# Six edits joined in a one-layer hybrid encoder: order at the start, bias tiles, residual rows, sine halves, sums of W_down

## The chip, the cores and the metric

The kernel runs on one core of a Trainium2 chip. TensorE (PE in the profile; PEld is its weight load) multiplies, VectorE (DVE) and ScalarE (ACT) move results out of PSUM and do the element work, GpSimd (POOL) does element work on SBUF and issues some DMAs, and SyncE (SP) issues most DMAs. Each engine runs its own queue of instructions in order. The metric is the time of one execution in microseconds (us), as the median of several runs; smaller is better.

## The reference

One encoder layer is applied to two inputs with shared weights, `x_sample` (512 rows) and `x_prompt` (1024 rows), each with 16 meta tokens in front. Width is 1024, the MLP has 4096 channels.

```python
def encoder_layer(x, ...):
    h = rmsnorm(x, g_mix)
    z = h @ w_in
    q, k, v, u, gate_na, gate_fn = jnp.split(z, ...)
    y_na = neighbourhood_attention(q, k, v, rel_bias, meta_bias) @ w_branch_na
    y_fn = fourier_mix(u) @ w_branch_fn
    mixed = jax.nn.sigmoid(gate_na) * y_na + jax.nn.sigmoid(gate_fn) * y_fn
    x = x + mixed @ w_out
    a = jax.nn.relu(rmsnorm(x, g_mlp) @ w_up)
    return x + (a * a) @ w_down
```

Attention has 8 heads of 64. A grid token sees a window of 8 rows by 16 columns of the 64-column grid with a relative bias, and all meta tokens. `fourier_mix` is the real part of a 2-D DFT over positions and the channels of each of four groups. At the end comes an RMSNorm, and the meta rows are dropped.

## The kernel before

All products are in float32, as three passes of float32r matmuls: each operand is split into a high part (a cast, mostly on ACT) and a low part (a subtraction on POOL or DVE), and `mm3` (L125) adds high x high, high x low and low x high in PSUM. `weights` (L145) is the usual way in: one DMA on SP, the cast on ACT, the low part on POOL unless told otherwise.

The program is written in Python without hardware loops. A scheduler orders every engine's queue when the kernel is built: by program order as priority, and by when it believes that an instruction is ready. Two helpers bend that order: `mark` (L103) finds the last instruction traced on some engines, and `behind` (L118) puts what follows behind them on the same engine; `pinned` (L114) does so for all engines. All waits between engines are made by the framework from the tiles that are read and written.

`run` (L350) does the sample first and then the prompt. For the sample:

- **Start** (L363 to L380). `read` (L277) loads the meta rows and four tiles of 128 rows through three buffers, norms each (ACT squares, DVE scales), and PE transposes it into `hT`. Value weights come in four quarters of 256 rows (`value_weights`, L299), their low parts on DVE. `qk_weights(0)` (L303) brings the first keys' and queries' weights, `tables` (L201) loads a window table, subtracts a mask and stores bias tables `g` in DRAM. `project_v` (L307) multiplies the meta rows first and then the four tiles and stores the values to DRAM (`vd`).
- **Attention** (`attention`, L513). `spread_v` (L753) copies the stored values within DRAM into the windows' order. `project(0)` (L537) makes keys and queries of the first pair of heads; its matmuls are lines L531 to L533. A `unit` (L628) fetches a bias tile (`bias`, L769: one or two DMAs from `g` and a POOL copy), does scores (L647, L648), softmax (L652 to L656), transposes (L660) and the product with the values (L680). Bias loads of head 0 stand behind `spread_v` on SP.
- **Gates** (`gates`, L783). One product per weight tile; a list `beside` names generators that take one step after each product, from the first number to before the second. `fold_u` (L248) multiplies the DFT over channels into W_u: its first step loads, its eight others use PE (L259) and store. `fold_positions` (L877) adds and subtracts mirrored positions.
- **merge_na** (L820): eight weight tiles of `w_na`, through two buffers `relu`; `fn_ahead` (L847) makes ready the other branch's weights. Then `fourier_channels` (L972), `fourier_positions` (L1033) with cosine and sine tables from DRAM (`sines`, L1026, one DMA on POOL's queue), and `merge_fn` (L915), which also begins to load `w_out`.
- **project_out** (L1084) loads the residual rows `acc`, adds the product with W_out and norms; `Up.run` (L1197) does W_up in 16 pairs of products. Beside them `reading` loads, norms and transposes the prompt's rows, one tile for each pair.

The prompt goes the same way; then `Halves` (L1223) does project_out and W_up, and `down` (L1610) does W_down for both inputs in a Strassen scheme of seven quarter products. A step `(n, u)` is product n with slice u of eight; it has six row tiles of six matmuls. `load(i)` (L1636) makes step i's weights: sums of up to four quarters on DVE (L1642), then the splits. In the last slice of a product, `evict` (L1711) takes each bank out, and `load(i + 2)` follows all six.

Of the kernel before, what the change touches and what calls it, by code (L numbers as in the profile page):

```python
# [17 lines left out]
F32 = mybir.dt.float32  # L18
# [8 lines left out]
D = 1024  # L27
# [41 lines left out]
class Layer:  # L69
    def __init__(self, tc, ctx, ins, outs):  # L70
# [16 lines left out]
        nc.sync.dma_start(self.sgn, ins["sgn"])  # L87
        self.small = ctx.enter_context(tc.tile_pool(name="small", bufs=4))
        self.wpool = ctx.enter_context(tc.tile_pool(name="w", bufs=2))
        self.wv = {}  # L90
        self.meta_values = None
# [109 lines left out]
    def tables(self, marks):  # L201
# [15 lines left out]
        with self.behind(marks):  # L217
            nc.sync.dma_start(mask, self.ins["colmask"])
            nc.sync.dma_start(win, self.ins["rel_win"])
# [78 lines left out]

    def value_weights(self, q, to=None, lo_engine=None, raw="raw"):  # L299
        return self.weights(self.ins["w_in"][q * 256:(q + 1) * 256, VC:VC + 512].rearrange("(kt p) c -> p kt c", p=128), to,  # L300
                            lo_engine=lo_engine, raw=raw)

    def qk_weights(self, pr, to=(None, None)):  # L303
        return (self.weights(self.rows("w_in", KCOL + pr * 128), to[0], lo_engine=self.nc.vector if pr else None),
                self.weights(self.rows("w_in", QC + pr * 128), to[1], scale=-DH ** -0.5))

    def project_v(self, name, T, hT, p, wv):  # L307
# [12 lines left out]
        for t in range(-1 if meta is None else 0, T // 128):  # L320
# [3 lines left out]
            self.mm3(ps[:n, :], [(hT[0][:, kt, pos:pos + n], hT[1][:, kt, pos:pos + n],  # L324
                                  wv[kt // 2][0][:, kt % 2, :], wv[kt // 2][1][:, kt % 2, :]) for kt in range(8)])
            vs = p.tile([128, 512], F32R, name="pt0", tag="pt0", bufs=self.ptb).bitcast(F32)
            nc.vector.tensor_copy(vs[:n], ps[:n])
# [22 lines left out]
    def run(self, order):  # L350
# [6 lines left out]
        for i, (name, T) in enumerate(order):  # L357
# [5 lines left out]
            if i == 0:  # L363
                with pool("first", "right") as p:
                    gain = p.tile([128, D], F32, name="gain")
                    reading = self.read(name, T, hT, lambda: p.tile([128, D], F32, name="xt", bufs=3),
                                        lambda: p.tile([128, D], F32, name="hn", bufs=2), gain)
                    next(reading)
                    next(reading)
                    for q in range(4):  # L370
                        next(reading, None)
                        self.wv[q] = self.value_weights(q, self.pair(p, [128, 2, 512], bufs=4), self.nc.vector, ("raw", "raw", "hi", "lo")[q])
                    marks = self.mark((mybir.EngineType.SP,))
                    w0 = self.qk_weights(0)

                    rest = self.tables(marks)
                    for _ in reading:
                        pass
# [40 lines left out]
            if small:  # L419
                wide = lambda: [fn.tile([128, n], F32R, name=f"wu{n}")[:, :1040].rearrange("p (a b) -> p a b", a=4) for n in (1040, 1072)]  # L420
                flat = lambda pair: [t.rearrange("p a b -> p (a b)") for t in pair]
                beside = [(self.fold_u(mp.tile([128, 512], F32, name="relu", bufs=2)[:, :128],
# [1448 lines left out]
```

## Time and profile before

| | us |
|---|---|
| runs | 1922.71, 1923.19, 1925.18 |
| median | 1923.19 |
| the profiled execution's own time | 1927.61 |
| its span, first to last instruction | 1925.8 |

The profile is of one execution. Part 1 of its page gives the busy time of each engine, the chain of waits goes back from the last instruction through whatever released each step, and a table of waits says for which engine's instruction or which DMA an engine stood idle (total us, times, longest). In rows of the timeline the first two numbers are start and duration in us, and the bracket is the idle time before and what ended it; "SPq" is a DMA issue on SP. Matmuls are pipelined, so the distance between starts and not the duration is a matmul's cost. Over the whole span the granted TensorE clock was 0.998 of full speed, and the DMAs moved 358.38 MB.

### The profile page before, as it was taken

The page shows a single profiled execution, that of the slowest core. Times are in us where ns is not written, and L with a number is a line of the kernel's source. Part 1 is how long each engine was busy: PE and PEld are TensorE (multiplying, and loading weights), DVE is VectorE, ACT ScalarE, POOL GpSimd, SP SyncE. Part 2 cuts the span into 40 slices and gives each one's busy share as a digit, 9 for nine tenths or more (in the row PEclk, how much of TensorE's full clock was granted, in tenths as well). Part 3 has the DMA queues.
Part 4 walks back from the last instruction along what each step waited for, and adds up shares of the span by engine and source line. Part 5 has one row for each costly group of instructions (what it writes and reads, how often), then busy time and mean ns, then how long its engine had stood idle before and what let it go on. Part 6 is the DMA issues. An engine that isn't in the chain of part 4 may idle for free.

```text
span 1925.8 us, 26107 instructions
## 1 busy us (share of the span) xinstructions
PE 1892.8 (98%) x9435; PEld 1588.0 (82%) x9435; DVE 1117.8 (58%) x1749; ACT 753.1 (39%) x1351; POOL 816.5 (42%) x674
## 2 busy tenths in 40 slices
PE   7999999999999999999999999999999999999998
PEld 5888888888888888888898878888888888888886
DVE  5771554787625567660427376656665326758856
ACT  3674333443315556541223234333333333333434
POOL 1335543455422233342233218887882323323531
PEclk9999999999999999999999999999999999999999
DMA  6757873687756455463452523444446778567733
GB/s 221 192 152 236 232 218 124 208 271 251 237 191 173 121 145 156 120 233 105 117 158 85 175 99 121 158 173 164 173 155 250 269 250 285 207 218 281 277 118 127
DMA packets 312945, 358.38 MB, mean 186 GB/s; under 512 B 51768, under 2 KB 222392, under 8 KB 312264
## 3 DMA queue, kind: packets, MB, share of 16 engines
q1 hardware_dynamic: 295056, 334.93, 53.0%
q0 software_dynamic: 17760, 21.80, 5.0%
q8 instruction: 74, 1.21, 0.3%
q14 instruction: 55, 0.45, 0.1%
HBM read 263.06 MB, written 96.16 MB: 187 GB/s over the span
## 4 chain that ended last, share of the span: by engine, by line
PE 89%; DMA 4%; DVE 2%; issue 2%; POOL 1%; ACT 1%; SPq 0%; POOLq 0%; DVEq 0%; ACTq 0%
PE ps_mm L132 23%; PE ps_o L132 22%; PE ps_s L132 19%; PE ps_t L132 11%; PE ps_mm L531 3%; PE ps_mm L532 3%; PE ps_mm L533 3%; PE ps_o L680 2%; PE ps_t L660 1%; DMA relu<-in_w_na 1%; DMA bm<-g_un 1%; DMA sin<-in_sin_prompt 1%; PE ps_s L648 1%; PE ps_s L647 1%; PE ps_t L194 0%
## 5 line engine op out<-in xcount | busy, mean ns | idle before, releaser
L157 POOL TENSOR_TENSOR w_lo<-w_raw,w_hi 128x1024 fp32r<-128x1024 f32 x69 | 177.1, 2567 | 217.9 <-ACT w_hi L155 151.9
L157 POOL TENSOR_TENSOR w_lo<-raw,w_hi 128x1024 fp32r<-128x1024 f32 (+1 forms) x49 | 100.0, 2044 | 202.1 <-ACT w_hi L155 196.2
L155 ACT CAST w_hi<-w_raw 128x1024 fp32r<-128x1024 f32 x88 | 92.5, 1051 | 180.1 <-PE ps_s L132 58.5
L157 DVE TENSOR_TENSOR h_lo<-long,h_hi 128x1024 fp32r<-128x1024 f32 x54 | 77.1, 1428 | 94.1 <-ACT h_hi L155 94.1
L531 PE MATMUL ps_mm<-hT,w_hi 128*128 128x512 f32 (+2 forms) x296 | 121.5, 410 | 0.0
L532 PE MATMUL ps_mm<-hT,w_hi 128*128 128x512 f32 (+2 forms) x296 | 110.4, 373 | 0.0
L533 PE MATMUL ps_mm<-hT,w_lo 128*128 128x512 f32 (+2 forms) x296 | 110.4, 373 | 0.0
L155 ACT CAST h_hi<-long 128x1024 fp32r<-128x1024 f32 x54 | 56.7, 1050 | 101.6 <-PE ps_s L132 25.1
L654 ACT ACTIVATE sc<-sc,ast 128x288 f32<-128x288 f32 (+4 forms) x96 | 53.9, 561 | 68.3 <-DVE ast L652 68.0
L155 ACT CAST w_hi<-raw 128x1024 fp32r<-128x1024 f32 (+1 forms) x49 | 40.9, 840 | 100.9 <-DVE raw L1642 54.4
L157 DVE TENSOR_TENSOR hs_lo<-short,hs_hi 128x512 fp32r<-128x512 f32 x54 | 72.3, 1339 | 13.9 <-ACT hs_hi L155 11.7
L1421 POOL TENSOR_TENSOR x<-w_hi,x 128x512 fp32r<-128x512 f32 (+1 forms) x39 | 64.9, 1663 | 18.4 <-ACT x L1418 18.4
L680 PEld LDWEIGHTS ps_o<-pt,vb 104*64 104x64 f32 (+6 forms) x576 | 62.4, 163 | 9.7 <-POOL vb L617 2.6
L132 PE MATMUL ps_t<-gate,x 128*128 128x512 f32 x276 | 66.5, 390 | 0.0
L533 PEld LDWEIGHTS ps_mm<-hT,w_lo 128*128 128x128 f32 x296 | 55.7, 188 | 10.4
L680 PE MATMUL ps_o<-pt,vb 104*64 104x128 f32 (+6 forms) x576 | 62.1, 243 | 1.9 <-POOL vb L617 1.2
L617 POOL TENSOR_TENSOR vb<-vr,vb 96x384 fp32r<-96x384 f32 (+4 forms) x48 | 48.6, 1031 | 34.7 <-ACT vb L616 34.7
L132 PE MATMUL ps_mm<-gate,x 128*128 128x512 f32 x256 | 63.2, 389 | 0.0
L774 POOL MEMSET bm<- 64x96 f32 (+2 forms) x64 | 11.2, 175 | 117.1 <-DVE ast L652 101.7
L132 PEld LDWEIGHTS ps_t<-gate,x 128*128 128x128 f32 x276 | 51.7, 188 | 10.9 <-ACT w_hi L136 0.2
L652 DVE CUSTOM_DVE_ANT_0 sc<-ps_s,bm 128x288 f32<-128x288 f32 (+4 forms) x96 | 46.4, 483 | 23.6 <-issue 10.7
L532 PEld LDWEIGHTS ps_mm<-hT,w_hi 128*128 128x128 f32 x296 | 56.2, 190 | 1.6
(714 smaller groups left out, 5574.4 us busy)
## 6 DMA issues: line engine op xcount, KB each, us to landing
long<-hidden_prompt SPq DMA_DIRECT2D x54, 512.0 KB
w_raw<-in_w_in SPq DMA_DIRECT2D x52, 512.0 KB
raw<-in_w_down SPq DMA_DIRECT2D x39, 512.0 KB
w_raw<-in_w_up SPq DMA_DIRECT2D x34, 512.0 KB
hidden_prompt<-h SPq DMA_DIRECT2D x32, 512.0 KB
short<-hidden_sample SPq DMA_DIRECT2D x54, 256.0 KB
w_lo<-in_w_down SPq DMA_DIRECT2D x18, 512.0 KB
w_raw<-in_w_out SPq DMA_DIRECT2D x16, 512.0 KB
```

Source lines behind the costliest of these rows:

```text
L132: self.nc.tensor.matmul(out, a, b, start=(i == 0 and not more), stop=(i == len(terms) - 1), skip_group_check=more)
L155: nc.scalar.copy(out=hi, in_=raw)
L157: (lo_engine or nc.gpsimd).tensor_tensor(out=lo, in0=raw, in1=hi.bitcast(F32), op=ALU.subtract)
L531: nc.tensor.matmul(ps, a[0], b[0], start=(kt == 0), stop=False)
L532: nc.tensor.matmul(ps, a[0], b[1], start=False, stop=False)
L533: nc.tensor.matmul(ps, a[1], b[0], start=False, stop=(kt == 7))
L617: nc.gpsimd.tensor_tensor(out=lo, in0=vs, in1=hi.bitcast(F32), op=ALU.subtract)
L647: nc.tensor.matmul(ps[:, :W], qs[hh][:, qc], ks[hh][:, 0, kw[0], kw[1]], start=True, stop=False)
L652: nc.vector.tensor_tensor_reduce(out=sc[:, :W], in0=ps[:, :W], in1=bm[:, :W], scale=1.0, scalar=3e38, op0=ALU.add, op1=ALU.min, accum_out= ...
L654: nc.scalar.activation(out=sc[:, :W], in_=sc[:, :W], func=AF.Exp, bias=st[:, 0:1], scale=-1.0, accum_out=st[:, 1:2])
L680: nc.tensor.matmul(po[:m, j * 128:(j + 1) * 128], v, x, start=(i == 0), stop=(i == len(ops) - 1))
L1421: (engine or self.nc.gpsimd).tensor_tensor(out=w[1], in0=raw, in1=w[0].bitcast(F32), op=ALU.subtract)
```

## The change

1. At the start `read` is replaced for the sample by `read_first`: the first 128 rows are SP's first load, the meta rows come after, row tiles 2 and 3 land in key buffers, and norms and splits are written out in one order. The load of `sgn` goes behind these loads. `project_v` does the meta rows next to last: high and low parts of their 16 columns side by side in one 48-column operand, 16 matmuls in place of 24, and one add. The keys' low part is on DVE behind the last transposes.
2. `first_bias` brings the bias tiles of the first six units ahead of the last values' store.
3. `fold_u` skips the step after the second gate product and ends one product later.
4. The residual rows' loads move from `project_out` to behind `fourier_positions`, pinned. The prompt's rows in `Up.run` are pinned too.
5. The prompt's second sine table is loaded in two halves of columns.
6. In `down`, the sums for the step after next are written between the evictions.

```diff
@@ -84,10 +84,10 @@
...
-        nc.sync.dma_start(self.sgn, ins["sgn"])
@@ -215,6 +215,7 @@
...
         with self.behind(marks):
+            nc.sync.dma_start(self.sgn, self.ins["sgn"])
             nc.sync.dma_start(mask, self.ins["colmask"])
@@ -296,12 +297,66 @@
...
+    def read_first(self, name, T, hT, gain, p, more):
...
+        xs, hns, raws = {}, {}, {}
+        def load(t):
+            n = NM if t < 0 else 128
+            xs[t] = p.tile([128, D], F32, name="xt", bufs=3) if t < 2 else more()
+            nc.sync.dma_start(xs[t][:n], self.ins["meta_tokens"] if t < 0 else self.ins[f"x_{name}"][t * 128:(t + 1) * 128, :])
+        def load_w(q):
+            raws[q] = self.wtile(("raw", "raw", "hi", "lo")[q], [128, 2, 512]).bitcast(F32)
+            nc.sync.dma_start(raws[q], self.value_rows(q))
+        def norm(t):
+            n = NM if t < 0 else 128
+            hns[t] = p.tile([128, D], F32, name="hn", bufs=2)
+            self.norm(xs[t][:n], gain, hns[t][:n], n)
+        def turn(t):
+            self.transpose_in(hns[t], hT, 0 if t < 0 else self.lead + t * 128, NM if t < 0 else 128)
+        def split(q):
+            self.wv[q] = self.split_sb(raws[q], *self.pair(p, [128, 2, 512], bufs=4), lo_engine=nc.vector)
+        load(0)
+        self.gain(gain, "g_mix")
+        load_w(0)
+        load(1)
+        load_w(1)
+        load(-1)
+        load_w(2)
+        load_w(3)
+        for t in range(2, T // 128):
+            load(t)
+        norm(0)
+        turn(0)
+        split(0)
+        norm(1)
+        split(1)
+        split(2)
+        turn(1)
+        split(3)
+        with self.behind(self.mark((mybir.EngineType.Activation, mybir.EngineType.DVE))):
+            norm(2)
+            turn(2)
+            for t in (-1, 3):
+                norm(t)
+                turn(t)
+    def value_rows(self, q):
+        return self.ins["w_in"][q * 256:(q + 1) * 256, VC:VC + 512].rearrange("(kt p) c -> p kt c", p=128)
...
-    def qk_weights(self, pr, to=(None, None)):
-        return (self.weights(self.rows("w_in", KCOL + pr * 128), to[0], lo_engine=self.nc.vector if pr else None),
...
+    def qk_weights(self, pr, to=(None, None), late=()):
+        return (self.weights(self.rows("w_in", KCOL + pr * 128), to[0], lo_engine=self.nc.vector if pr or late else None, lo_marks=late),
                 self.weights(self.rows("w_in", QC + pr * 128), to[1], scale=-DH ** -0.5))
@@ -317,14 +372,35 @@
...
-        for t in range(-1 if meta is None else 0, T // 128):
+        order = list(range(T // 128))
+        for t in order if meta is not None else order[:-1] + [-1] + order[-1:]:
+            if meta is None and t == T // 128 - 1:
+                with self.behind(self.mark((mybir.EngineType.SP,))):
+                    self.first_bias(p, T)
...
             ps = self.psum()
-            self.mm3(ps[:n, :], [(hT[0][:, kt, pos:pos + n], hT[1][:, kt, pos:pos + n],
-                                  wv[kt // 2][0][:, kt % 2, :], wv[kt // 2][1][:, kt % 2, :]) for kt in range(8)])
+            if t < 0:
+                own = p.tile([128, 512], F32R, name="pt1", tag="pt1", bufs=self.ptb)[:, :8 * 48].rearrange("p (k c) -> p k c", k=8)
+                nc.gpsimd.tensor_copy(own[:, :, NM:2 * NM].rearrange("p k (g c) -> p k g c", c=8),
+                                      self.zero[:, None, None, 0:8].to_broadcast([128, 8, 2, 8]))
+                for i in range(2):
+                    nc.scalar.copy(out=own[:, :, 32 * i:32 * i + NM], in_=hT[i][:, :, 0:NM].bitcast(F32))
+                for i in range(2):
+                    for kt in range(8):
+                        nc.tensor.matmul(ps[:48], own[:, kt], wv[kt // 2][i][:, kt % 2, :], start=(kt + i == 0), stop=(kt + i == 8))
+            else:
+                self.mm3(ps[:n, :], [(hT[0][:, kt, pos:pos + n], hT[1][:, kt, pos:pos + n],
+                                      wv[kt // 2][0][:, kt % 2, :], wv[kt // 2][1][:, kt % 2, :]) for kt in range(8)],
+                         late="b" if meta is None and t < 2 else "a")
             vs = p.tile([128, 512], F32R, name="pt0", tag="pt0", bufs=self.ptb).bitcast(F32)
-            nc.vector.tensor_copy(vs[:n], ps[:n])
+            if t < 0:
+                low = p.tile([128, 512], F32R, name="pt1", tag="pt1", bufs=self.ptb).bitcast(F32)[:n]
+                nc.scalar.copy(out=low, in_=ps[32:32 + n])
+                nc.vector.tensor_tensor(out=vs[:n], in0=ps[:n], in1=low, op=ALU.add)
+            else:
+                nc.vector.tensor_copy(vs[:n], ps[:n])
@@ -363,19 +439,12 @@
...
-                    reading = self.read(name, T, hT, lambda: p.tile([128, D], F32, name="xt", bufs=3),
-                                        lambda: p.tile([128, D], F32, name="hn", bufs=2), gain)
-                    next(reading)
-                    next(reading)
-                    for q in range(4):
-                        next(reading, None)
-                        self.wv[q] = self.value_weights(q, self.pair(p, [128, 2, 512], bufs=4), self.nc.vector, ("raw", "raw", "hi", "lo")[q])
+                    self.read_first(name, T, hT, gain, p, lambda: att.tile(
+                        [128, 2, T // 64 + 2, 64], F32R, name="k", tag="k", bufs=4).rearrange("p i a b -> p (i a b)").bitcast(F32)[:, :D])
                     marks = self.mark((mybir.EngineType.SP,))
-                    w0 = self.qk_weights(0)
+                    w0 = self.qk_weights(0, late=self.mark((mybir.EngineType.DVE,)))
                     rest = self.tables(marks)
@@ -419,10 +488,10 @@
...
-                beside = [(self.fold_u(mp.tile([128, 512], F32, name="relu", bufs=2)[:, :128],
+                beside = [self.fold_u(mp.tile([128, 512], F32, name="relu", bufs=2)[:, :128],
                                        [t.bitcast(F32) for _ in range(2) for t in flat(self.pair(mp, [128, 2, 512]))],
-                                       lambda: flat(self.pair(fn, [128, 4, 128], bufs=4))), 0, 9),
-                          (fold, 5, 13)]
+                                       lambda: flat(self.pair(fn, [128, 4, 128], bufs=4)))]
+                beside = [(*beside, 0, 1), (*beside, 2, 10), (fold, 5, 13)]
@@ -454,6 +523,10 @@
             with self.pinned():
                 for _ in ahead:
                     pass
+                if small:
+                    acc = [ap.tile([128, D], F32, name=f"acc{t}") for t in range(T // 128)]
+                    for t in range(T // 128):
+                        nc.sync.dma_start(acc[t], self.ins[f"x_{name}"][t * 128:(t + 1) * 128, :])
@@ -501,6 +573,15 @@
...
+    def first_bias(self, p, T):
+        blocks = row_blocks(T // 64)
+        wide = max(b["n"] * w for b in blocks for w in KW)
+        for u in range(6):
+            h, R, j = u // (4 * len(blocks)), u // 4 % len(blocks), u % 4
+            self.bms.append(p.tile([128, wide], F32, name="bm", bufs=6))
+            self.bias(self.bms[-1], h, j, KW[j], blocks[R])
@@ -637,9 +718,12 @@
...
-            bm = p.tile([128, wide], F32, name="bm", bufs=6 if T == 512 else 4)
-            with self.behind(spread if h == 0 else []):
-                self.bias(bm, h, j, w, b)
+            if self.bms:
+                bm = self.bms.pop(0)
+            else:
+                bm = p.tile([128, wide], F32, name="bm", bufs=6 if T == 512 else 4)
+                with self.behind(spread if h == 0 else []):
+                    self.bias(bm, h, j, w, b)
@@ -1027,7 +1111,9 @@
...
-        self.nc.gpsimd.dma_start(t, self.ins[f"sin{i}_{name}"].rearrange("(t p) k -> p t k", p=128))
+        src = self.ins[f"sin{i}_{name}"].rearrange("(t p) k -> p t k", p=128)
+        for ks in (slice(0, 262), slice(262, R + 1)) if i and R > 512 else (slice(0, R + 1),):
+            self.nc.gpsimd.dma_start(t[:, :, ks], src[:, :, ks])
@@ -1081,14 +1167,12 @@
...
         gain = self.gain(p.tile([128, D], F32, name="gain", bufs=1), "g_mlp")
-        for t in range(nt):
-            nc.sync.dma_start(acc[t], x[t * 128:(t + 1) * 128, :])
@@ -1217,7 +1301,8 @@
...
                 if g:
-                    next(reading, None)
+                    with layer.pinned():
+                        next(reading, None)
@@ -1634,12 +1719,17 @@
...
         def load(i):
+            for _ in load_parts(i):
+                pass
+        def load_parts(i):
             if i >= len(steps):
                 return
             rs, rl, rw, *rest = (x.bitcast(F32) for x in self.raws.pop(i))
             n, u = steps[i]
             for x, (_, sign) in zip(rest, self.parts(self.DOWN[n][1], u)[1:]):
                 nc.vector.tensor_tensor(out=rw, in0=rw, in1=x, op=ALU.add if sign > 0 else ALU.subtract)
+                yield
@@ -1767,13 +1857,21 @@
...
+            loading, sums = iter(()), 0
+            if u == nu - 1 and i + 2 < len(steps):
+                loading = load_parts(i + 2)
+                sums = len(self.parts(self.DOWN[n + 1][1], 1)) - 1
             for t in range(nh):
                 product(banks[t], t, n, [u])
                 if u == nu - 1:
                     evict(n, t)
+                    if t < sums:
+                        with layer.pinned():
+                            next(loading, None)
             with layer.pinned():
                 if u == nu - 1:
-                    load(i + 2)
+                    for _ in loading:
+                        pass
```

More of the change, by code (lines that the diff above doesn't have):

```diff
@@ L90, in __init__ @@
         self.wv = {}
+        self.bms = []
         self.meta_values = None
@@ L297, in read @@
         self.transpose_in(*last)
+    def read_first(self, name, T, hT, gain, p, more):
+        nc = self.nc
+        xs, hns, raws = {}, {}, {}
[38 more added lines that the diff above has]
+                turn(t)
@@ L299, in value_weights @@
+    def value_rows(self, q):
+        return self.ins["w_in"][q * 256:(q + 1) * 256, VC:VC + 512].rearrange("(kt p) c -> p kt c", p=128)
     def value_weights(self, q, to=None, lo_engine=None, raw="raw"):
-        return self.weights(self.ins["w_in"][q * 256:(q + 1) * 256, VC:VC + 512].rearrange("(kt p) c -> p kt c", p=128), to,
-                            lo_engine=lo_engine, raw=raw)
-    def qk_weights(self, pr, to=(None, None)):
-        return (self.weights(self.rows("w_in", KCOL + pr * 128), to[0], lo_engine=self.nc.vector if pr else None),
+        return self.weights(self.value_rows(q), to, lo_engine=lo_engine, raw=raw)
@@ L365, in run @@
                     gain = p.tile([128, D], F32, name="gain")
-                    reading = self.read(name, T, hT, lambda: p.tile([128, D], F32, name="xt", bufs=3),
-                                        lambda: p.tile([128, D], F32, name="hn", bufs=2), gain)
-                    next(reading)
-                    next(reading)
-                    for q in range(4):
-                        next(reading, None)
-                        self.wv[q] = self.value_weights(q, self.pair(p, [128, 2, 512], bufs=4), self.nc.vector, ("raw", "raw", "hi", "lo")[q])
+                    self.read_first(name, T, hT, gain, p, lambda: att.tile(
+                        [128, 2, T // 64 + 2, 64], F32R, name="k", tag="k", bufs=4).rearrange("p i a b -> p (i a b)").bitcast(F32)[:, :D])
                     marks = self.mark((mybir.EngineType.SP,))
-                    w0 = self.qk_weights(0)
+                    w0 = self.qk_weights(0, late=self.mark((mybir.EngineType.DVE,)))
                     rest = self.tables(marks)
-                    for _ in reading:
-                        pass
                     self.project_v(name, T, hT, att, self.wv)
@@ L480, in run @@
                 continue
-            acc = [ap.tile([128, D], F32, name=f"acc{t}") for t in range(T // 128)]
             self.short = mlp = self.Up(self, ap, hp_, mp, name, T, h2T)
@@ L485, in run @@
                 rest = list(wout)
-            self.project_out(hp_, mp, self.ins[f"x_{name}"], T, h2T, rest, acc, mlp, marks)
+            self.project_out(hp_, mp, T, h2T, rest, acc, mlp, marks)
             out.close()
@@ L1082, in out_weights, with project_out @@
             yield self.weights(src, place and (place() if callable(place) else self.pair(*place)), lo_engine=self.nc.vector if i == 2 else None)
-    def project_out(self, hp, p, x, T, m, wo, acc, mlp, marks):
+    def project_out(self, hp, p, T, m, wo, acc, mlp, marks):
         nc = self.nc
```

## The prediction

> **What bounds the kernel now.** First the page, part 1, then the waits of PE alone, then the chain of waits for the pace of a matmul.
>
> ```profile
> PE 1892.8 (98%) x9435; PEld 1588.0 (82%) x9435; DVE 1117.8 (58%) x1749; ACT 753.1 (39%) x1351; POOL 816.5 (42%) x674
> ```
> ```profile
> PE ps_t L194 <- DVE hn L184: 8.1, 1, 8.1
> PE ps_t L194 <- DVE st L181: 2.6, 1, 2.6
> PE ps_t L660 <- DVE sc L656: 2.1, 4, 1.0
> PE ps_s L132 <- ACT hid_hi L155: 2.1, 1, 2.1
> PE ps_mm L132 <- DVE w_lo L157: 1.8, 1, 1.8
> PE ps_o L680 <- POOL vb L617: 1.2, 4, 0.5
> PE ps_t L132 <- POOL w_lo L157: 1.2, 1, 1.2
> PE ps_mm L259 <- DMA w_hi<-in_w_uT: 1.0, 1, 1.0
> PE ps_o L132 <- DMA sin<-in_sin_prompt: 1.0, 1, 1.0
> PE ps_t L660 <- DVE pt L137: 1.0, 2, 0.5
> PE ps_t L194 <- DVE gate L137: 0.9, 1, 0.9
> ```
> ```profile
> 444.31 5.44 PE ps_mm L132 x24
> ```
>
> PE is busy 1892.8 of 1925.8 us, so all the time to be won without taking matmuls away is 33.0 us. The waits say where it lies: 8.1 + 2.6 + 1.8 us in the first 26 us, and after that single waits of 1 to 2 us, far apart. Everything between them is matmuls, one every 5.44 / 24 = 0.227 us. So an edit is worth the PE wait that it ends, and no more; work taken off another engine is worth nothing by itself. Each part below is matched with one of these rows.
>
> **The start (value projection, keys and queries).** The first fence has the chain of waits, the second the timeline, the third 10-us windows (columns: PE, PEld, DVE, ACT, POOL busy).
>
> ```profile
> 0.76 0.39 SPq L87
> ...
> 2.13 5.87 DMA xt<-in_x_sample
> ...
> 57.66 7.19 DMA bm<-g_un
> ```
> ```profile
> 3.29 1.05 ACT L178 ACTIVATE hn<-xt 16x1024 f32<-16x1024 f32 x1 [1.05 <-DMA xt<-in_meta_tokens]
> ...
> 11.69 1.94 PE L194 MATMUL ps_t<-ident,hn 128*128 128x128 f32 x8 [2.62 <-DVE st L181]
> ...
> 21.81 2.39 POOL L157 TENSOR_TENSOR w_lo<-w_raw,w_hi 128x1024 fp32r<-128x1024 f32 x1 [19.26 <-ACT w_hi L155]
> 21.96 3.32 DVE L157 TENSOR_TENSOR w_lo<-w_lo,w_hi 128x1024 fp32r<-128x1024 f32 x1
> ...
> 47.47 0.29 PE L531 MATMUL ps_o<-hT,w_hi 128*128 128x272 f32 x1
> ```
> ```profile
> 0.00:10.00 10.00, 1.00 (x8) 0.93 (x8) 3.56 (x14) 4.91 (x11) 1.98 (x14) 1.00 0.73 234
> 10.00:20.00 10.00, 8.31 (x33) 5.62 (x34) 9.10 (x20) 8.73 (x17) 0.00 (x0) 1.00 0.88 299
> 20.00:30.00 10.00, 8.16 (x44) 5.00 (x44) 9.97 (x12) 4.80 (x7) 2.39 (x1) 1.00 0.68 210
> ```
>
> Before, SP issues sgn (L87), the meta rows, the gain and only then, at 2.13, the first 128 rows. They land at 8.00, and their transposes start at 11.69, 3.7 us later. After the change these rows are SP's first load, at 0.76, the place of sgn. When do they land? Lower end: the 64 KB meta load, issued at 0.76 + 0.39, about 1.2, was there at 3.29, so 2.1 us; the other 448 KB at the window's 234 GB/s take 2.0 us; landing at 4.9. Upper end: the 5.87 us of the old load, landing at 6.7. I take 5.2, near the lower end, since nothing stands ahead of the load any more. Plus the same 3.7 us of norm: transposes at 8.9, **2.8 us sooner** (1.3 to 3.1).
>
> The meta tile needs 16 matmuls in place of 24: 8 x 0.227 = **1.8 us** less PE work. Its price is three copies of 16 rows (ACT, POOL), in a stretch where these have room, and a read of 16 rows by ACT ahead of DVE's add; none is on PE.
>
> In the stretch 21.8 to 25.3 DVE takes 3.32 us for the last value weight's low part while POOL does the same kind of job for the key weights. With K's low part on DVE behind the last transposes, POOL is quiet there, and the wait of **1.8 us** ends. But DVE is the engine to watch: it is busy 3.56 + 9.10 + 9.97 = 22.6 us of the first 30. Its work until the last tile is transposed stays about that (less some 2 us of slowed low part, plus 1.2 for K). Started 2.8 us sooner it ends near 28. PE has the last tile's 5.44 us still to do behind that, which gives 33.4 as DVE's bound, while PE's own bound is 47.47 - 2.8 - 1.8 - 1.8 = 41.1. So DVE has 7 us in hand if the order is good. Start: 2.8 + 1.8 + 1.8 = **6.4 us**. Bounds: 1.3 + 1.8 - 1.0 (a new wait for low parts) = 2.1, and 3.1 + 1.8 + 3.5 (all PE idle time of the windows 10 to 30) = 8.4.
>
> Sgn, mask and window table now go behind these loads. They feed the bias tables only. Row tiles 2 and 3 land in key buffers, so SP no longer stands still between their loads.
>
> **Bias tiles ahead of the last values' store.** Before, a bias load of the first units is issued only at 57.66, behind the values' spreading; it lands 7.19 us later, at 64.9, a softmax waits for it, and PE waits 1.0 us for that (the longest in the row of L656). Six bias loads now stand before the last store on SP's queue. They wait for the table's store, so the last store, the spreading and the first values are queued behind that. I take **1.0 us** won; bounds -2.0 (table late by 2 us) and 1.3.
>
> **fold_u one gate later.**
>
> ```profile
> 157.55 1.07 PE L132 MATMUL ps_s<-hT,w_hi 128*128 128x512 f32 x4
> 159.66 0.46 PE L259 MATMUL ps_mm<-relu,w_hi 128*128 128x128 f32 x2 [1.04 <-DMA w_hi<-in_w_uT]
> ```
>
> The next gate had begun, so its weights are there; only the fold waits for its load. One gate later (5.44 us) the load has landed: **1.0 us** (0 to 1.2). What is late next: fold_u also ends 5.4 us later, and with it one of the two buffers that the w_na loads use.
>
> **Residual rows.** Four loads of 512 KB, which no one needs before project_out, now stand behind the DFT and the last fn weights.
>
> ```profile
> L1091 SPq DMA_DIRECT2D acc<-in_x_sample x4: 482/682/858, 229.2 to 234.3; - x4
> ```
> ```profile
> 236.84 9.68 DMA relu<-in_w_na
> ```
> ```profile
> 248.00:250.00 2.00, 2.00 (x8) 1.55 (x7) 0.00 (x0) 0.00 (x0) 1.20 (x2) 0.71 0.27 79
> 250.00:252.00 2.00, 2.00 (x8) 1.70 (x7) 0.47 (x1) 0.00 (x0) 0.00 (x0) 0.50 0.33 72
> ```
> ```profile
> 277.46 1.05 ACT L155 CAST w_hi<-w_raw 128x1024 fp32r<-128x1024 f32 x1 [2.15 <-DMA w_raw<-in_w_out]
> ```
>
> The last w_na load takes 9.68 us because 2.1 MB of rows were issued just ahead; PE waits 2.1 us for it. Then comes a second loss: the granted clock falls to 0.5 after the wait. What PE loses by it is 0.29 of one 2-us window and 0.50 of the next, 1.6 us. At 234 GB/s the rows are 9 us of transfer; at any rate seen they are more than the 2.1 that is missing, so both go: 3.7. What comes back: the rows now travel with the first w_out load, whose cast at 277.46 already waits for its landing, and ACT holds the fn weights' casts behind it. Six to nine us of rows against the few us until merge_fn needs these: I take -0.5 (0 to -3). Residual: **3.2 us** (0.7 to 3.7).
>
> The Trainium skill, page "TensorE: Matmul & The Clock Gate", Part 1, says that the clock falls back after at least one idle window of about 3.4 us. Here it fell after a wait of 2.1 us, so the trace disagrees on the length. By the page the dip has another cause and would stay.
>
> **Sine table in halves.**
>
> ```profile
> 989.81 10.99 DMA sin<-in_sin_prompt
> ```
> ```profile
> 989.81 0.88 POOL L1030 DMA_DIRECT2D sin<-in_sin_prompt  x1 [10.50 <-PE ps_mm L132]
> ```
>
> PE reaches the table's use 1.0 us before the load lands at 1000.80. The first chunk's matmuls read columns 0 to 261 only, so half the bytes free them; half of 10.99 ends at 995.3, and even three quarters at 998.1. The other half is needed a chunk later. Price: one more issue of 0.9 us on POOL, which had been idle for 10.5 us. **1.0 us** (0 to 1.2).
>
> **W_down's sums.**
>
> ```profile
> 1721.83 1.22 DVE raw L1642
> ```
>
> In the step before the t4 quarter's second one, three sums of 1.22 us, ACT's cast and POOL's low part come in a row after the last of six evictions, and PE waits 1.2 us. The evictions are 6 matmuls, 1.36 us, apart, so between them the sums start five products, 6.8 us, sooner. An eviction and a sum together are longer than 1.36, so DVE falls behind, but by less than three sums, 3.7 us, and PE comes back to a bank only a step of 8.2 us later. At least 3 us are won for a wait of 1.2: **1.2 us** (0 to 1.4).
>
> **Prompt rows pinned into the Up loop.**
>
> ```profile
> 348.85 1.28 DVE r L184
> ```
>
> The norm of a prompt row, hoisted, stands on DVE ahead of the split for which PE waits 0.9 us. Pinned behind the second pair of Up products it cannot: **0.9 us** (-1 to 1.0).
>
> Sum: 6.4 + 1.0 + 1.0 + 3.2 + 1.0 + 1.2 + 0.9 = **14.7 us**. The profiled execution took 1927.61 us (span 1925.8 and 1.8 around it), so it would take 1912.9; it lies 4.4 above the median of the runs, 1923.19, and from that I predict **1908.5 us**. The low ends sum to 2.1 - 2 + 0 + 0.7 + 0 + 0 - 1 = -0.2, or 1923.4, the high ends to 8.4 + 1.3 + 1.2 + 3.7 + 1.2 + 1.4 + 1.0 = 18.2, or 1905.0.
>
> **Rivals.**
> *The start stays with DVE.* DVE is above 9 of 10 us busy from 10 to 30; if its static order puts norms ahead of the low parts, PE stands and the start gives its low end, 2.1: 14.7 - 4.3 = 10.4, 1912.8. Chance 0.18.
> *The rows collide with w_out.* Then the residual edit gives 0.7: 12.2, 1911.0. Chance 0.10.
> *The dip stays.* The clock's fall has another cause than this wait: 1.6 less, 1910.1. Chance 0.05.
> *The halves are not seen as halves*, if the dependence is kept on the whole tile: 1.0 less, 1909.5. Chance 0.04.
> *New waits take the place of the old.* The order of all engines is made anew, and 1-us waits reappear where another engine is next; the meta matmuls, 1.8, and some 1.4 of the rest stay won: 1920. For it: ten small waits lie in the attention rows L660 and L680 now. Against: each named wait has one releaser, which is moved. Chance 0.09.
> *Slower: pinned rows hold ACT.* Each of eight pinned steps issues a 512 KB load and puts the norm's square on ACT. If ACT's order has it closer than the load's time (5.87 us at the start), relu evictions and weight casts queue behind. Of each product's 5.44 us ACT spends 1.05 on a cast and about as much on an eviction, so 3.3 are to spare; where ACT waits longer for the rows, PE stands. At the whole 5.87 that is 2.6 us, with the 1.6 of the clock 4.2, in eight steps 33.6: 1942. Against: the steps were there before and PE shows no such wait. Chance 0.04.
>
> **How the numbers follow.** Forecast 0.50, with 1905 to 1912 as its own range; all rivals but the last two are faster too. A measurement of this kernel tells about 0.2%, 3.8 us, from no change. Faster 0.50 + 0.18 + 0.10 + 0.05 + 0.04 = 0.87; within 0.09; slower 0.04. The range 1903 to 1917 leaves out the last two cases and some of the tails.
>
> **What would show it.** Right: the first 128-row transposes at about 9 and L531's first matmul near 41; no L194, w_lo, hid_hi, in_w_uT or in_sin_prompt row of 1 us among PE's waits; granted clock 1.00 around the last w_na weight; the step after the three sums without POOL's wait. Wrong: L531 after 45; a PE wait for fn weights or w_out before project_out; ACT waiting for prompt rows more than the few us it did.

## The result, and the profile after

The changed kernel takes **1937.85 us** (median of 6 runs, 1935.87 to 1939.36) against 1923.04 (6 runs, 1922.33 to 1925.18) for the kernel before on the same chip: a ratio of 1.0074 with a 95% interval of 1.0061 to 1.0087. It is slower, by 0.7%, and 29 us above the forecast of 1908.5.

The profiled execution took 1938.8 us, its span is 1937.0. Part 1 of its page, and then its waits of PE (total us, times, longest):

```profile
PE 1895.2 (98%) x9427; PEld 1590.5 (82%) x9427; DVE 1108.1 (57%) x1750; ACT 754.8 (39%) x1354; POOL 810.3 (42%) x675
```
```profile
PE ps_t L194 <- DVE r L184: 19.1, 8, 3.8
PE ps_t L194 <- DVE hn L184: 8.6, 2, 8.3
PE ps_t L744 <- DVE sc L740: 1.2, 3, 0.4
PE ps_o L764 <- POOL vb L698: 1.2, 4, 0.5
```

Most of the rows on which the prediction rested are gone: no `w_lo`, no `st`, no `in_w_uT`, no `hid_hi`, no `in_sin_prompt`. In their place stands one that was not there: eight waits, 19.1 us, of the transposes (L194) for a normed prompt row `r` (L184). They all lie in the sample's Up loop. The window of that stage in the changed kernel (us, then busy time and instructions of PE, PEld, DVE, ACT, POOL, then granted clock, DMA share and GB/s):

```profile
350.00:500.00 150.00, 130.85 (x580) 106.87 (x579) 98.04 (x123) 53.95 (x84) 65.81 (x33) 0.95 0.71 228
```

PE stands for 19.15 of these 150 us, and the granted clock is 0.95. The timeline of PE there, six of the eight groups of transposes:

```profile
374.32 1.94 PE L194 MATMUL ps_t<-ident,r 128*128 128x128 f32 x8 [3.40 <-DVE r L184]
390.42 1.07 PE L194 MATMUL ps_t<-ident,r 128*128 128x128 f32 x8 [1.50 <-DVE r L184]
403.45 1.71 PE L194 MATMUL ps_t<-ident,r 128*128 128x128 f32 x8 [3.78 <-DVE r L184]
...
433.13 1.06 PE L194 MATMUL ps_t<-ident,r 128*128 128x128 f32 x8 [2.60 <-DVE r L184]
...
462.82 1.06 PE L194 MATMUL ps_t<-ident,r 128*128 128x128 f32 x8 [2.59 <-DVE r L184]
479.71 1.06 PE L194 MATMUL ps_t<-ident,r 128*128 128x128 f32 x8 [2.20 <-DVE r L184]
```

From 374.32 to 479.71 are seven intervals, 15.06 us each on average. Two products of 24 matmuls at 0.227 us are 10.9, and eight transposes take about 1 more. So a pair pays some 3 us on average, and that is the loss. Most of it is the 19.1 us of waits; three stretches at a clock of 0.5, 13.7 us together (last section), cost about half their length beside it, some 6 us by our estimate. The chain of waits, from the first row's load and then through one such interval, tells what PE waits for:

```profile
364.19 4.96 DMA r<-in_x_prompt
...
390.34 6.84 DMA r<-in_x_prompt
397.26 0.09 ACT r L178
...
399.78 2.02 DVE st L182
401.82 0.17 DVE st L183
402.01 1.30 DVE r L184
403.31 0.14 issue
403.45 1.71 PE ps_t L194 x8
```

In the interval the row is loaded, normed and transposed one after the other, from 390.34 to 403.45, and PE comes to the transposes 3.78 us too soon. Little stands between: a weight's cast on ACT holds the norm's square root back by some 0.8 us (398.41 to 399.26, not shown), and the step at 399.78 takes 2.02 us, where it took 0.21 at 371.97, for a reason that was not looked into. The issues on SP's queue just behind that show where the next load stands:

```profile
403.93 0.37 SPq L1252 DMA_DIRECT2D hidden_sample<-hid_lo  x1
405.31 0.37 SPq L1260 DMA_DIRECT2D hidden_sample<-hn  x1
405.73 0.50 SPq L1273 DMA_DIRECT2D acc<-in_w_down  x1
406.27 0.68 SPq L1274 DMA_DIRECT2D acc<-in_w_down  x1
407.00 0.46 SPq L289 DMA_DIRECT2D r<-in_x_prompt  x1
```

The one row buffer was free at 402.01 + 1.30 = 403.3, but the load is held to its place behind the stores of the pair's second product (L1252, L1260), which wait for the evictions of that product, and behind `combine`'s loads: 3.7 us later.

The start did move. The timeline of the changed kernel has the first 128-row transposes and the first product of the keys:

```profile
8.30 1.94 PE L194 MATMUL ps_t<-ident,hn 128*128 128x128 f32 x8 [8.30 <-DVE hn L184]
...
43.11 0.29 PE L612 MATMUL ps_o<-hT,w_hi 128*128 128x272 f32 x1
```

That is 3.4 us and 4.4 us earlier than before.

### The profile page after: what moved, and what is told of

Read it like the earlier page. It is cut to its first block, busy times and chain, and to the rows that moved or that the text cites. A ratio compares the mean times of both kernels' runs of the same rounds, so it can differ in the third digit from the quotient of the medians.

```text
span 1937.0 us, 26118 instructions
## 1 busy us (share of the span) xinstructions
PE 1895.2 (98%) x9427; PEld 1590.5 (82%) x9427; DVE 1108.1 (57%) x1750; ACT 754.8 (39%) x1354; POOL 810.3 (42%) x675
## 4 chain that ended last, share of the span: by engine, by line
PE 90%; DVE 3%; DMA 2%; issue 2%; ACT 2%; POOL 0%; SPq 0%; POOLq 0%; DVEq 0%; ACTq 0%
PE ps_mm L132 22%; PE ps_o L132 22%; PE ps_s L132 18%; PE ps_t L132 11%; PE ps_mm L612 3%; PE ps_mm L613 3%; PE ps_mm L614 3%; PE ps_o L764 2%; PE ps_t L744 1%; DMA r<-in_x_prompt 1%; PE ps_t L194 1%; DVE hid_lo L1248 1%; PE ps_s L731 1%; PE ps_s L732 1%; DVE r L184 1%
## 5 line engine op out<-in xcount | busy, mean ns | idle before, releaser
L157 POOL TENSOR_TENSOR w_lo<-w_raw,w_hi 128x1024 fp32r<-128x1024 f32 x68 | 171.0, 2515 | 244.5 <-ACT w_hi L155 132.6
L157 DVE TENSOR_TENSOR hs_lo<-short,hs_hi 128x512 fp32r<-128x512 f32 x54 | 65.9, 1220 | 16.6 <-ACT hs_hi L155 14.5
L155 ACT CAST w_hi<-raw 128x1024 fp32r<-128x1024 f32 (+1 forms) x49 | 41.1, 840 | 65.3 <-PE ps_mm L132 15.3
```

The lines of the kernel that those rows point to most:

```text
L155: nc.scalar.copy(out=hi, in_=raw)
L157: (lo_engine or nc.gpsimd).tensor_tensor(out=lo, in0=raw, in1=hi.bitcast(F32), op=ALU.subtract)
```

## The experiments

Each kernel was timed with the kernel before on the same chip; ratios are to that. Three theories stood at first. A: one row buffer makes load, norm and transposes follow each other, the norm's place is late, and PE stands at the transposes. B: the order of the Up stage, made anew by the other edits, is at fault. C: ACT's queue is held by the row loads. Two lines of `Up.run` are at issue:

```python
                if g:
                    with layer.pinned():
                        next(reading, None)
```

**Is it this edit?** First the changed kernel with these steps free, and the kernel before with only these steps pinned.

```diff
-                    with layer.pinned():
-                        next(reading, None)
+                    next(reading, None)
```

> The changed kernel with the prompt's row steps in Up.run not pinned (as before); all else of the change stays. Theory A (one row buffer: load, norm and transposes of a tile follow each other, about 16 us pinned against a pair of products of 11.75 us, and PE stands at the transposes): the waits of PE L194 for DVE r L184 (19.1 us, and some 7 us of halved clock) go, time 1911 (1908 to 1914), 0.6% under before. Rival B (the order of the Up stage was remade by the other edits and the pins only show it): stays above 1930 and PE waits elsewhere between 350 and 500 us. Rival C (ACT's queue held by row loads, casts and evictions late): 1911 as well, but then the changed kernel's PE waits should have been for ACT, not for DVE r.

> The kernel before with nothing but the prompt's row steps pinned. Theory A: 1923 + 23 to 27 = 1946 to 1950, with eight waits of PE L194 for DVE r. Rival B: within 4 us of 1923.

Free: **1914.21 us** (1913.02 to 1915.02), ratio 0.9948 (0.9936 to 0.9961). Pinned alone in the kernel before: 1949.46 (1948.6 to 1949.84), ratio 1.0132 (1.0118 to 1.0146). The window of the stage in the first kernel, and the wait of PE in the second:

```profile
350.00:500.00 150.00, 150.00 (x703) 125.17 (x702) 118.05 (x134) 60.81 (x90) 84.96 (x40) 1.00 0.80 256
```
```profile
PE ps_t L194 <- DVE r L184: 18.6, 8, 3.6
```

PE does 703 matmuls in place of 580 in the same 150 us. The pinned reading costs 23.6 us (1937.85 - 1914.21) in one kernel and 25.6 (1949.46 - 1923.88) in the other, so it does not need the other five edits. Rival B falls. The free kernel is at the upper edge of what theory A expected (1908 to 1914).

**Which queue?** A pinned step fixes four things: the row's load on SP, the norm on ACT and DVE, the transposes on PE. They were held one by one; the marks name the engines. A rival, D, came in here: the load's late place on SP's queue makes the loss, whatever order the norm has.

```diff
-                    with layer.pinned():
+                    with layer.behind(layer.mark((mybir.EngineType.PE,))):
```

> The changed kernel with the row steps pinned on PE alone: transposes keep their place behind the pair of products, loads and norms are free. If the norm's late place on ACT and DVE makes the chain long (theory A, first form): a load of 5 to 7 us and a norm of 3.5 us fit into 11.75 us, so within 3 us of the unpinned kernel, 1911 to 1914. If PE's fixed place alone is the cause (second form): 1930 or more, with the same eight waits.

> The changed kernel with the reading's steps held to a fixed place on SP's queue alone (the 512 KB row load), the norm and the transposes free. Theory A (the norm's late place on ACT and DVE, together with the single row buffer, makes the 24 us): the load waits for its buffer and not for SP, so 1914 us (1911 to 1917) and no PE wait for r. Rival D (the load's late place makes it: the row lands late, and whatever order the norm has, it follows): 1930 us or more, with PE waits for r of some us each.

> The changed kernel with the reading's steps held to a fixed place on ACT and DVE alone (the norm), the row load on SP and the transposes on PE free. Theory A: the norm stands behind the evictions of the second pair of products, its tile's buffer comes free only behind it, and the next load with it; eight intervals of some 15 us between transposes in place of 11.75: 1936 us (1930 to 1942). Rival D (the load's place on SP): with the load free 1914 us (1911 to 1918).

> The changed kernel with the reading's steps held to their place on ACT, DVE, POOL and PE, the row load on SP alone free; one row buffer. Theory D (the load's place on SP behind the store of the second product makes the whole loss): 1914 us (1912 to 1916), first row load at about 330 us, no PE wait for r over 1 us. Theory A, as far as it is left (a late norm and a late place of the transposes together, though each alone cost nothing): 1930 us or more.

| held to its place on | us | ratio (interval) |
|---|---|---|
| nothing | 1914.21 | 0.9948 (0.9936 to 0.9961) |
| PE | 1913.91 | 0.9948 (0.9933 to 0.9963) |
| ACT, DVE | 1915.01 | 0.9952 (0.9938 to 0.9965) |
| ACT, DVE, POOL, PE | 1913.91 | 0.9945 (0.9930 to 0.9960) |
| SP | 1938.16 | 1.0071 (1.0057 to 1.0085) |
| all | 1937.85 | 1.0074 (1.0061 to 1.0087) |

Our first theory, A, had the norm's late place on ACT and DVE as the cause. It expected 1914 of SP alone and 1936 of ACT and DVE alone, and both came out the other way round. The place of one DMA issue for each step, on SP, makes the whole loss, as long as there is one row buffer. C falls with A: where ACT is held, nothing is lost. The waits of PE for `r` with SP alone held, and with all but SP held:

```profile
PE ps_t L194 <- DVE r L184: 18.7, 8, 3.6
```
```profile
PE ps_t L194 <- DVE r L184: 0.4, 1, 0.4
```

**Lateness, or the single buffer?** Two row buffers in turn, each row loaded one step ahead, all steps pinned as in the changed kernel (the diff shows this version); then the same with the first row's load in a step of its own, earlier and not held to a place; then this early first load with one buffer.

```diff
+        def load(t):
+            loaded[t] = xts(t)
+            nc.sync.dma_start(loaded[t], x[t * 128:(t + 1) * 128, :])
...
+            if t + 1 < T // 128:
+                load(t + 1)
...
-                reading = self.read(*nxt, hT, lambda: tile_("r0").bitcast(F32), lambda: tile_("r2").bitcast(F32), tile_("r3").bitcast(F32))
+                reading = self.read(*nxt, hT, lambda t: tile_(f"r{t % 2}").bitcast(F32), lambda: tile_("r2").bitcast(F32), tile_("r3").bitcast(F32))
```

> The changed kernel, still pinned on all engines, with two row buffers in turn and each row tile loaded one step ahead. Theory A: only the norm, some 5 us, is left between the pair's end and the next transposes, so PE waits for r of under 0.5 us each; 1909 to 1913, beside the unpinned kernel. If the pin itself costs: 1920 or more.

> Two row buffers, each row loaded a step ahead, all steps held to their place (1920.5 us), and now the first row's load a pair of products earlier too. Theory A: the two waits of the first tile that are left (4.8 us together) and the half-clock window behind them (1.7 us) go: 1914 us (1911.5 to 1916). If the 350-us wait for a gate's split, which is gone with fixed places, is worth its 0.9 us, it is at or under the kernel without fixed places on the same chip. Rival B (the order of the Up stage made anew costs the rest, whatever the waits for r): 1919 to 1921.

> The changed kernel, one row buffer, all steps held to their place, but the first row's load issued a pair of products earlier. Theory D1 (a closed chain: each later load stands on SP behind the second product's store and waits for the one buffer, its norm and the transposes follow, and PE's wait delays the next store): only the first of eight rounds is mended, the others stay near 14.5 us apart in place of 11.8, 1931 to 1936 us, with six or seven PE waits for r. Theory D2 (only the first load is late, some 35 us behind that of the free kernel, and the rest is dragged along): 1914 to 1919 us, at most two waits for r.

Two buffers: 1920.46 us (ratio 0.9981, 0.9972 to 0.9990). That misses the 1909 to 1913 of theory A and would fit "the pin itself costs", but two waits of the first tile, 4.8 us, are left. With the first load early too, all steps after it still pinned, they go, and so does the rest: **1914.11** (0.9949, 0.9936 to 0.9963). One buffer with the early first load: 1935.52 (1.0056, 1.0039 to 1.0073). Their waits of PE, in this order:

```profile
PE ps_t L194 <- DVE r L184: 4.8, 2, 3.7
```
```profile
PE ps_t L194 <- DVE r L184: 0.5, 1, 0.5
```
```profile
PE ps_t L194 <- DVE r L184: 17.3, 8, 4.1
```

The issues of the row loads, first with one buffer, an early first load and all later steps pinned, then with all engines but SP held:

```profile
329.63 0.33 SPq L289 DMA_DIRECT2D r<-in_x_prompt  x1
...
367.89 1.06 PE L194 MATMUL ps_t<-ident,r 128*128 128x128 f32 x8 [0.41 <-DVE r L184]
...
374.88 0.73 SPq L289 DMA_DIRECT2D r<-in_x_prompt  x1
...
388.22 0.52 SPq L289 DMA_DIRECT2D r<-in_x_prompt  x1
```
```profile
330.09 0.33 SPq L289 DMA_DIRECT2D r<-in_x_prompt  x1
...
368.36 0.35 SPq L289 DMA_DIRECT2D r<-in_x_prompt  x1
...
376.58 0.33 SPq L289 DMA_DIRECT2D r<-in_x_prompt  x1
```

In both the first row has been normed by about 368 (its transposes start at 367.89 and 368.4), so its buffer is free. Free on SP, the second load goes out there, at 368.36; in its place behind the second product's store, at 374.88, 6.5 us later. From there it is a closed chain: load, norm, transposes, products, their evictions and stores, and the next load behind these. An early first load mends one round of eight; a load one step ahead opens the chain. At 1914 us this version, like that with free steps, is faster than both kernels; the two cannot be told apart. With SP alone free, all seven later loads go out within 0.1 us of the norm that frees the one buffer, and nothing is lost; so the one buffer by itself costs nothing. In the changed kernel three of the seven do so too, such as that at 390.34, as the norm at 388.99 + 1.29 frees the buffer; three others, at 407.00, 436.68 and 467.22, go out 3.7, 3.7 and 4.5 us after it, and one, at 374.83, 0.6. A load that late is no loss by itself: with all steps free three loads also go out 3.3 us after the norm that frees their buffer, but there the norms end 1.2 to 4.6 us before the transposes start. How the rest of the loss divides between these late loads' further effects and the order that the scheduler gave the norms around them was not separated.

**The sizes of the other edits**, undone one at a time in the kernel with free steps: the residual rows' loads back in `project_out`; the old start with the old place of the bias tiles; the old place of the bias tiles alone.

```diff
-                    self.first_bias(p, T)
```

> The kernel without the fixed places of the prompt's rows (1914.2 us) and with the residual rows' four loads back in project_out. The prediction's term says +3.2 us (0.7 to 3.7), 1917.4, with a PE wait of about 2 us for the last merge_na weight and a half-clock window behind it. Rival E (the wait and the clock window of the profiled execution before were not in the typical one, so the term is at most 1 us): 1914 to 1915.3, with a wait under 1 us and no clock window near it.

> The kernel without the fixed places of the prompt's rows (1914.2 us) and with the whole start of before: reading in the old order, 24 matmuls for the meta rows, keys' low part on POOL, bias tiles behind the values' store. The prediction's terms for start and bias tiles say +7.4 us, 1921.6, with first transposes at 11.7 and L531's first counterpart at 47.5 instead of 43.4. Rival F (the start won only what the first key products show, 4.1 to 4.4 us, and the bias tiles nothing): 1918.3 to 1919. Above 1920 decides for the terms, below 1919.5 for F.

> The kernel without the fixed places of the prompt's rows (1914.2 us) and with the bias tiles of the first six units again behind the values' spreading. The prediction's term says +1.0 us, 1915.2, with a PE wait of about 1 us among those for the softmax at the first unit. Rival F (the last store and the spreading, queued behind the bias loads, cost as much as these win): 1914.0 to 1914.5.

The kernel with free steps was not timed on the chips of these three, so another of its speed stands in for it. Rows back: 1916.52 us (0.9962, 0.9950 to 0.9975), 2.4 above the 1914.11 of the two-buffer kernel on the same chip; the time lies between what the term and rival E expected, and the waits, 0.70 and 0.44 us without a fall of the clock, are as E said. Old start: 1919.36 (0.9976, 0.9967 to 0.9986), 5.4 above the 1913.91 of the kernel with all but SP held, on its chip; that is under the 1919.5 set for rival F, but F also gave the bias tiles nothing. Old bias tiles alone: 1918.51 (0.9972, 0.9961 to 0.9984), 4.6 above the same 1913.91. We had expected 1 us of the last at most. The timeline and the windows of that kernel:

```profile
61.77 0.40 PE L728 MATMUL ps_s<-k,q 128*128 128x288 f32 x1 [2.26 <-DVE ast L733]
```
```profile
62.00:64.00 2.00, 2.00 (x14) 1.93 (x14) 0.68 (x4) 1.31 (x6) 0.56 (x2) 0.79 0.64 170
64.00:66.00 2.00, 1.65 (x9) 1.36 (x8) 1.62 (x8) 0.78 (x4) 0.56 (x3) 0.50 0.77 176
```

The first softmax step, in the kernel before and then in this one:

```profile
63.62 0.38 DVE L652 CUSTOM_DVE_ANT_0 sc<-ps_s,bm 128x216 f32<-128x216 f32 x1 [0.46 <-DMA bm<-g_un]
```
```profile
61.33 0.38 DVE L733 CUSTOM_DVE_ANT_0 sc<-ps_s,bm 128x216 f32<-128x216 f32 x1 [2.58 <-DMA bm<-g_un]
```

With the new start PE is at the first units some 4 us earlier, while the first bias tile comes only 2.3 us earlier; the softmax waits for the tiles longer, PE with it, and the clock falls to half behind that wait. So a new start without early bias tiles wins 0.9 us (1919.36 - 1918.51, within the spread of the runs), and both together 5.4. Early bias tiles with the old start were not run, so the 4.6 is their worth behind the new start alone.

## Why the prediction was wrong

**The step that failed** is "Prompt rows pinned into the Up loop", forecast at 0.9 us won (-1 to 1.0) and measured at 23.6 us lost. It looked at one wait, at 350 us, which the hoisted norm of the first row imposes on a gate's split. That wait does go when the step is pinned. But a pinned step issues a 512 KB load as well, and the step was not followed to SP's queue. The trace of before had the row that speaks against it, which the prediction did not read. The view of the tile `r` in the kernel before (count, least, median and largest ns, start of the first and of the last):

```profile
L194 PE MATMUL ps_t<-ident,r x64: 270/272/276, 378.9 to 462.1; 128*128 128x128 f32 x64
...
L288 SPq DMA_DIRECT2D r<-in_x_prompt x8: 332/379/862, 340.4 to 448.0; - x8
```

The first load is at 340.4 and the first transposes at 378.9, so it ran 38 us ahead of its user. In the changed kernel it is at 364.19, 10.1 us ahead. But this first lead is not the loss: the early first load with one buffer gave it back and still took 1935.52 us. From the third row on the lead is 12 to 15 us in both kernels. What differs is the order in each round, here in the kernel before:

```profile
389.47 0.41 SPq L288 DMA_DIRECT2D r<-in_x_prompt  x1
```
```profile
390.72 1.03 PE L194 MATMUL ps_t<-ident,r 128*128 128x128 f32 x8
```

Before, from the third load on, each load goes out 0.75 to 3.3 us ahead of the transposes of the row before it, and PE never waits for a norm. In the changed kernel the loads go out from 0.1 us ahead of these transposes to 4.4 us behind them (374.83 against 374.32, 407.00 against 403.45), and PE waits at every one.

**The slower rival**, given 0.04 and 1942 us, named the place, and its time is near. Its mechanism does not stand: it had ACT's queue held by the rows. With ACT and DVE held the time is 1915.01; the price comes from SP, and PE pays it at the transposes themselves. (It also had an eviction of this stage cost ACT about as much as a cast, 1.05 us; the rows show 0.58.) "The steps were there before and PE shows no such wait" was no argument, since before they were free to run ahead.

**The other terms** hold in the profiled executions and come to some 70% in the medians. Without the pinned rows the prediction comes to 13.8 us; the profiled executions give 1927.61 - 1914.56 = 13.0. Of medians it is 9.7 (1923.88 - 1914.21):

| term | forecast | measured, medians |
|---|---|---|
| start and bias tiles | 6.4 + 1.0 | 5.4 |
| residual rows | 3.2 | 2.4 |
| fold_u, sine halves, W_down's sums | 3.2 | not run alone; the rest, 1.9 |
| prompt rows pinned | 0.9 | -23.6 |

PE's waits named for the three edits of the third row (1.0, 1.0 and 1.2 us) are gone from the page. The start was forecast to bring L531's first matmul to 41.1 and brought it to 43.1; the first transposes came at 8.3 where 8.9 was forecast. Of its three parts the earlier transposes came (3.4 us for 2.8), PE has the 8 matmuls less (9427 against 9435) and the wait for `w_lo` is gone; still 2 us of the sum are missing at the first keys, some 1.2 of them in new short waits (0.9 of PE for `hT`, 0.3 for `hn`). The rest was not followed. The remark "wrong: L531 after 45" does not apply.

The second error is in the baseline. The prediction took the 4.4 us by which the profiled execution lay over the median as something that the changed kernel would keep. The one profiled execution with free steps lay 0.35 over its median (1914.56 against 1914.21). Part of what the edits removed was only in that one execution: with the residual rows where they were, the wait for the last w_na weight was 2.1 us with a clock window behind it, but the kernel before with only the prompt rows pinned, which loads the residual rows as before, has 0.8 us there and a clock of 1.00:

```profile
PE ps_s L132 <- ACT hid_hi L155: 0.8, 1, 0.8
```

The kernel with rows back shows two shorter waits too. Its timeline of PE:

```profile
235.68 0.50 PE L132 MATMUL ps_mm<-oT_hi,hid_hi 128*128 128x512 f32 x1 [0.70 <-ACT hid_hi L155]
...
239.15 0.50 PE L132 MATMUL ps_s<-oT_hi,hid_hi 128*128 128x512 f32 x1 [0.44 <-ACT hid_hi L155]
```

Without the failed step and with that baseline corrected, the forecast would have been 1923.2 - 13.8 + 4, some 1913 to 1914. That is hindsight: the 4 is taken from the result.

**Rivals that can be judged.** "The start stays with DVE" gave the start its low end, 2.1, and the bias tiles 1.0; together they won 5.4, and where the start won less, 0.9, the bias tiles held it and not DVE. "The rows collide with w_out" falls: 2.4 of 3.2 were won. "The halves are not seen as halves" falls too: PE's wait for `in_sin_prompt`, 1.0 us before, is gone. "New waits take the place of the old" was right in kind and wrong in place and size: one new wait, eight times.

## What to carry to other kernels

To hold a step to its place, list what the step issues on every queue, loads above all, and look up in the trace between which other steps these go out now. Where the new place is behind work that itself waits for the step, move the load a step ahead into a second buffer before the rest is held. An edit that brings work forward is worth only what the next input allows: measure it together with the edit that brings that input. And subtract no distance between one profiled execution and the median, unless its waits are known to be in the others too.

## What the runs showed of the hardware

The clock. The windows of the changed kernel in which the granted clock begins to fall, three times in the stage:

```profile
372.00:374.00 2.00, 0.00 (x0) 0.00 (x0) 2.00 (x6) 0.80 (x1) 0.00 (x0) 0.75 1.15 349
...
402.00:404.00 2.00, 0.55 (x4) 0.58 (x5) 1.95 (x3) 0.00 (x0) 0.00 (x0) 0.93 0.37 101
```
```profile
434.00:436.00 2.00, 2.00 (x8) 1.56 (x7) 1.93 (x5) 0.87 (x2) 0.00 (x0) 0.61 0.81 265
```

and those in which it comes back:

```profile
378.00:380.00 2.00, 2.00 (x6) 1.54 (x6) 0.94 (x1) 0.60 (x1) 1.47 (x1) 0.55 0.67 273
...
406.00:408.00 2.00, 2.00 (x8) 1.57 (x7) 0.50 (x1) 0.00 (x0) 0.00 (x0) 0.72 0.92 289
```
```profile
436.00:438.00 2.00, 2.00 (x7) 1.57 (x6) 0.16 (x1) 0.17 (x1) 0.00 (x0) 0.54 1.06 332
```

At a clock of 0.5 from the fall on, a mean of 0.75 puts the fall at 373.0, 0.93 at 403.7 and 0.61 at 434.4; in the same way the clock is back at 379.8, 407.1 and 437.8, so a stretch at half clock lasts 3.4 us, or 6.8 in the first case. The distances of the falls are 30.7 and 30.7, nine times 3.41 us. In the kernel before with the rows pinned the same windows put the falls at 384.2, 411.6 and 442.3, eight and nine times 3.41 apart. So within an execution the falls lie on a fixed grid, and a grid window is 3.41 us. With it the waits above can be sorted. The wait of 2.60 us that ends at 433.13 has 2.1 us in one grid window (431.0 to 434.4), and the clock falls; that of 2.59 which ends at 462.82 is cut at 461.7 into 1.5 and 1.1, and it does not. In the kernel before, the wait of 2.07 us that ends at 247.29 has 1.9 us in the window up to the fall at 248.8; in that with the rows pinned, one of 2.41 us that ends at 471.30 has 1.7 us in the window up to 473.0, and the clock stays at 1.00. So what counted here was not the length of a wait, but how much of one grid window was idle: 1.7 us were not enough, 1.9 were. In the first microseconds the granted clock is no guide: it shows 1.00 there, but the eight transposes at 8.30 in the changed kernel take 1.94 us, as those at 374.32 with a clock of 0.5, and not 1.06, as those at 462.82 with 1.00.

The Trainium skill, page "TensorE: Matmul & The Clock Gate", Part 1, has such a free-running window of 3413 ns, and the grid agrees. It also says that the clock falls back after at least one idle window; in these runs some 1.9 us of idle time within one were enough, so for the length the measurement decides. The rival "the dip stays", drawn from that page of the Trainium skill, is not borne out: where the last w_na weight comes in time, in the kernel with free steps, the granted clock is 1.00 in all windows from 236 to 264 us.
